# A state-space stage whose matrix products take a fixed place behind the large products

## The chip, the core and the metric

The kernel runs on one core of a Trainium2 chip. The metric is the device time of one execution in microseconds (us), here the median of three runs. A core has five instruction queues that run on their own and meet at semaphores: TensorE (PE, matrix products), VectorE (DVE), ScalarE (ACT), GpSimd (POOL) and SyncE (SP, which here only issues transfers, and waits for what each of them needs before it goes on to the next).

## The reference

One layer of a decoder block, 512 tokens of width 1024, everything in float32:

```
h = RMSNorm(x);  u = h @ W_in                     # 11512 columns: three mixers and three gates
y_A = DSA(u_A) @ W_br_A                           # attention over the 256 top keys
y_B = NSA(u_B) @ W_br_B                           # compressed, selected and window attention
y_C = SSD(u_C) @ W_br_C                           # state-space mixer, Mamba-2
x = x + (sig(g_A)*y_A + sig(g_B)*y_B + sig(g_C)*y_C) @ W_out
x = x + relu(RMSNorm(x) @ W_1)^2 @ W_2
```

The state-space mixer works on 4 chunks (c) of 128 tokens, 4 groups (g) and 8 heads of 64 channels in a group:

```
cb     = C[chunk] @ B[chunk].T                    # 128x128, one for each group
lmat   = exp(a_cum_i - a_cum_j), j <= i           # 128x128 for each head: the decay
y_diag = (cb * lmat) @ (dt * xs)                  # inside the chunk
states = B.T @ (decay * dt * xs)                  # what the chunk hands on
h_c+1  = h_c * chunk_decay + states               # the recurrence over chunks
y_off  = (C @ h_c) * exp(a_cum)                   # from the chunks before
y      = RMSNorm((y_diag + y_off + xs * D) * silu(z)) * g
```

## The kernel before

Two generators write the program. `main` goes through the latency-bound work: the index scores of DSA, the DSA attention, the state-space stage (`ssd`), the NSA attention. `filler` holds the large products: all columns of `W_in`, then the branch products with `W_br`. Each large product is three matrix instructions of 128x512 (`mm3`, L364 to L367, since a float32 is split into a high and a low half); they are the "products" of this text. `main` yields a price in ns; the loop at the end of `build_kernel` then takes steps of `filler` until their prices make up for it. A stage multiplies its prices by a ratio: R1 for DSA, R3 for the state-space stage, R2 for NSA. Where `main` yields a name instead ("x2"), the filler runs until that part is done. `main` is written with a higher priority (HM), so the scheduler, which puts each engine's instructions into one fixed order by its own estimate of when inputs are ready, may draw an instruction of `main` ahead of filler work written earlier. On the chip each engine then keeps that order.

The filler's gates: the branch products begin once NSA has begun its second group of queries ("att2"), those of the state-space branch once that stage is done ("yc"), the last of the NSA branch (`b1`) once the NSA output has been written and read back: its first half needs "nsa5", its second half "nsa". If the filler stands at a gate, it yields None, and `main` goes on alone.

The state-space stage (L1118 to L1242) has 16 units (g, c), taken in pairs of groups. `stage1` takes buffers and issues the six loads of a unit: E (L1130, 512 KB, the cumulated decay of 8 heads, broadcast to 128 partitions), xs (L1132) and zs (L1134), 256 KB each, and bcx, three tiles of 64 KB (L1136 to L1138). All have two buffers. `stage2` has the product C B (L1145, PSUM "pT", evacuated to cbm by ACT), the mask on E (POOL, L1148), eight exponentials (ACT, L1151), the scaled inputs xt and xw (POOL), and E times cbm (DVE, L1158). `stage3` has the product with the carried state (L1169), the new state (L1176), the eight y products (L1186) and the evacuation yv; four transposes of yv (L1197) follow one unit later. The loop calls `need(i + 2)`, then `stage2(i + 1)`, then `stage3(i)`, so loads are written two units ahead.

The NSA attention (L784 to L1000) has 32 units of four heads: scores (L801, L802), row maximum (DVE, L803), exponentials (ACT, L810), the scaling (DVE, L823), transposes (L837), their evacuation into a high and a low half (ACT L841, DVE L842), the product with V (L849, L850), and every second unit an output (ACT L856, DVE L857, write L858), which `load_y` (L714 to L716) reads back and splits for `b1`.

Of the kernel before, what the change touches and what calls it, by code (L numbers as in the profile page):

```python
# [7 lines left out]
F32 = mybir.dt.float32  # L8
# [26 lines left out]
R0, R1, R2, R3 = 1000.0, 1.5, 2.5, 0.5  # L35


def build_kernel(ctx, tc, A, out):
    nc = tc.nc
# [35 lines left out]
    bt_d = scratch("bt_d", [S, 512])  # L75
# [288 lines left out]
    def mm3(o, lh, ll, rh, rl, first, last):  # L364
        pe.matmul(o, lh, rh, start=first, stop=False)  # L365
        pe.matmul(o, lh, rl, start=False, stop=False)  # L366
        pe.matmul(o, ll, rh, start=False, stop=last)  # L367
# [750 lines left out]
    def ssd(sv, ratio):  # L1118
# [5 lines left out]
        def stage1(g, c):  # L1124
            u = U()
            u.g, u.c = g, c
            rows = slice(c * 128, c * 128 + 128)
            cols = slice(g * 512, g * 512 + 512)
            u.E = sp.tile([128, 8, 128], F32, name="E", bufs=2)
            nc.sync.dma_start(u.E, bcast_rows(ac_d, c * 32 + g * 8, 8))  # L1130
            u.xs = sp.tile([128, 512], F32, name="xs", bufs=2)
            nc.sync.dma_start(u.xs, xs_d[rows, cols])  # L1132
            u.zs = sp.tile([128, 512], F32, name="zs", bufs=2)
            nc.sync.dma_start(u.zs, zs_d[rows, cols])  # L1134
            u.b = sp.tile([128, 3, 128], F32, name="bcx", bufs=2)
            nc.sync.dma_start(u.b[:, 0], bt_d[rows, g * 128:g * 128 + 128])  # L1136
            nc.sync.dma_start(u.b[:, 1], BC_d[g * 128:g * 128 + 128, rows])
            nc.sync.dma_start(u.b[:, 2], BC_d[512 + g * 128:512 + g * 128 + 128, rows])  # L1138
            return u

        def stage2(u):
# [3 lines left out]
            pe.matmul(p[:, :128], u.b[:, 1], u.b[:, 2], start=True, stop=True)  # L1145
# [17 lines left out]
        def stage3(u):  # L1163
# [3 lines left out]
            if c:  # L1167
                po = ps("sc", [128, 512])
                pe.matmul(po, u.b[:, 2], hst[g], start=True, stop=True)  # L1169
# [4 lines left out]
            if c < 3:  # L1174
                pst = ps("pT", [128, 512])
                pe.matmul(pst, u.b[:, 0], u.xw, start=True, stop=True)  # L1176
# [8 lines left out]
            for h in range(8):  # L1185
                pe.matmul(py[:, h * 64:h * 64 + 64], u.E[:, h], u.xt[:, h * 64:h * 64 + 64], start=True, stop=True)  # L1186
# [7 lines left out]
            def tr():  # L1194
                pt = ps("pT", [128, 4, 128])
                for k in range(4):
                    pe.transpose(pt[:, k], yv[:, k * 128:k * 128 + 128], ident)  # L1197
# [18 lines left out]
        yield from need(0)  # L1216
        yield from need(1)
        yield from stage2(us[0])
        for i in range(16):
# [6 lines left out]
            yield from stage3(us[i])  # L1226
        TR.pop()()
# [362 lines left out]
```

## Time and profile before

| | |
|---|---|
| median of 3 runs | 1424.58 us (1424.15 to 1425.3) |
| the profiled execution's own time | 1425.82 us |
| its span in the trace | 1424.1 us |
| PE busy, of the span | 1365.5 us, 96% |
| DVE, ACT, POOL busy | 1044.6, 712.6, 347.0 us |
| mean granted clock of PE | 0.987 |
| moved by the transfers | 195.92 MB, 138 GB/s over the span |

An instruction's busy time on PE overlaps that of the next, so a busy PE says only that it never stood still. What it cost to stand still is in the idle time, given in brackets in the timeline and in the list of waits, with the instruction that ended it. The granted clock is the share of full speed: 1.00 is 2.4 GHz, 0.50 is 1.2 GHz.

### The profile page before, as it was taken

The numbers are of one execution on the slowest core, as the hardware profiler recorded it, in microseconds if no ns is written. First come the engines' busy times: TensorE is split into PE (matmuls) and PEld (weight loads), VectorE is DVE, ScalarE is ACT, GpSimd is POOL, SyncE is SP. The second block draws the span as 40 slices with busy tenths as digits, with TensorE's granted clock in tenths as the row PEclk, the third lists the DMA queues.
The fourth block names the chain that finished last, engine by engine and source line by source line (L and its number), as shares of the span: only waits on it lengthen the run. The fifth ranks groups of instructions, "written<-read, shape, count | busy, mean of one in ns | idle before, by whom it ended". The sixth has DMA issues, their size and how long they took to land.

```text
span 1424.1 us, 19720 instructions
## 1 busy us (share of the span) xinstructions
PE 1365.5 (96%) x6760; PEld 1126.1 (79%) x6760; DVE 1044.6 (73%) x1959; ACT 712.6 (50%) x1433; POOL 347.0 (24%) x294
## 2 busy tenths in 40 slices
PE   5989899999999999999999999999799999999998
PEld 4878688888877877788888867787579888888887
DVE  4599966798977665468568898888655777869841
ACT  5445245677666566455555544646433444443420
POOL 5454201111046576202003533524100000000000
PEclk9999899999999999999999999999999999999999
DMA  6236465544576778844326743424464433241221
GB/s 204 73 102 139 130 189 144 137 113 125 133 224 190 215 202 223 232 139 122 96 79 193 228 134 87 136 67 126 158 212 127 126 111 110 87 136 45 67 89 52
DMA packets 232097, 195.92 MB, mean 138 GB/s; under 512 B 17200, under 2 KB 183484, under 8 KB 231996
## 3 DMA queue, kind: packets, MB, share of 16 engines
q1 hardware_dynamic: 226524, 183.12, 44.3%
q0 software_dynamic: 4608, 8.39, 2.2%
q10 hardware_dynamic: 864, 3.15, 0.6%
q8 instruction: 53, 0.87, 0.3%
q14 instruction: 48, 0.39, 0.1%
HBM read 157.85 MB, written 36.77 MB: 137 GB/s over the span
## 4 chain that ended last, share of the span: by engine, by line
PE 71%; DVE 10%; DMA 7%; issue 4%; ACT 4%; POOL 2%; SPq 2%; DVEq 0%; ACTq 0%; POOLq 0%
PE pj L365 17%; PE pj L366 17%; PE pj L367 16%; PE sc L366 3%; PE sc L367 3%; PE sc L365 3%; PE pT L837 2%; PE sc L802 2%; PE sc L801 2%; PE pv L850 2%; PE pv L849 2%; DVE wlo L159 1%; DMA gld<-g_d 1%; SPq L525 1%; DMA E<-ac_d 1%
## 5 line engine op out<-in xcount | busy, mean ns | idle before, releaser
L158 ACT ACTIVATE whi<-wraw 128x1024 fp32r<-128x1024 f32 (+3 forms) x188 | 181.7, 975 | 210.8 <-PE pj L366 124.3
L159 DVE TENSOR_TENSOR wlo<-wraw,whi 128x1024 fp32r<-128x1024 f32 (+1 forms) x164 | 194.5, 1188 | 77.4 <-ACT whi L158 75.6
L365 PE MATMUL pj<-hTh,whi 128*128 128x512 f32 x384 | 154.9, 403 | 0.2 <-DVE cacc L732 0.2
L367 PE MATMUL pj<-hTh,wlo 128*128 128x512 f32 x384 | 153.5, 400 | 0.0
L366 PE MATMUL pj<-hTl,whi 128*128 128x512 f32 x384 | 153.3, 399 | 0.0
L365 PE MATMUL pj<-whi,hTh 128*128 128x512 f32 (+2 forms) x352 | 141.6, 404 | 8.3 <-DVE stk L435 3.2
L810 ACT ACTIVATE p<-p,nb,rs 128x256 f32<-128x256 f32 (+3 forms) x192 | 123.2, 645 | 50.6 <-DVE nb L808 50.6
L366 PE MATMUL pj<-wlo,hTh 128*128 128x512 f32 (+2 forms) x352 | 140.0, 398 | 0.8 <-POOL wlo L159 0.8
L367 PE MATMUL pj<-whi,hTl 128*128 128x512 f32 (+2 forms) x352 | 138.5, 394 | 0.0
L365 PE MATMUL pj<-yh,whi 128*128 128x512 f32 x256 | 103.0, 406 | 9.4 <-ACT yh L715 7.7
L366 PE MATMUL pj<-yl,whi 128*128 128x512 f32 x256 | 102.2, 399 | 0.4 <-DVE yl L716 0.4
L367 PE MATMUL pj<-yh,wlo 128*128 128x512 f32 x256 | 101.9, 399 | 0.0
L366 PE MATMUL pj<-h2l,whi 128*128 128x512 f32 (+1 forms) x256 | 96.3, 376 | 0.0
L367 PE MATMUL pj<-h2h,wlo 128*128 128x512 f32 (+1 forms) x256 | 96.2, 376 | 0.0
L365 PE MATMUL pj<-h2h,whi 128*128 128x512 f32 (+1 forms) x256 | 96.1, 376 | 0.0
L821 POOL TENSOR_TENSOR p<-p,rc 128x256 f32<-128x256 f32 (+3 forms) x48 | 38.2, 795 | 219.7 <-DVE rc L816 63.2
L365 PEld LDWEIGHTS pj<-whi,hTh 128*128 128x128 f32 x352 | 68.3, 194 | 22.5 <-issue 6.4
L365 PEld LDWEIGHTS pj<-hTh,whi 128*128 128x128 f32 x384 | 72.3, 188 | 16.4 <-issue 1.7
L367 PEld LDWEIGHTS pj<-hTh,wlo 128*128 128x128 f32 x384 | 72.2, 188 | 15.2 <-issue 1.2
L366 PEld LDWEIGHTS pj<-hTl,whi 128*128 128x128 f32 x384 | 72.3, 188 | 15.0 <-issue 1.7
L841 ACT ACTIVATE pth<-pT 128x512 fp32r<-128x512 f32 x95 | 55.0, 593 | 56.8 <-PE pT L837 54.8
L366 PEld LDWEIGHTS pj<-wlo,hTh 128*128 128x128 f32 x352 | 68.4, 194 | 14.9 <-issue 2.2
(357 smaller groups left out, 3372.9 us busy)
## 6 DMA issues: line engine op xcount, KB each, us to landing
wraw<-in_w_in_dram SPq DMA_DIRECT2D x84, 512.0 KB, 4.5
wraw<-in_w_ff_dram SPq DMA_DIRECT2D x40, 512.0 KB, 4.1
gld<-g_d SPq DMA_DIRECT2D x48, 256.0 KB, 3.3
qd<-in_w_ff_dram SPq DMA_DIRECT2D x24, 512.0 KB, 3.9
q_d<-qev SPq DMA_DIRECT2D x128, 64.0 KB, 2.6
qu<-q_d POOLq DMA_DIRECT2D x32, 256.0 KB, 3.7
E<-ac_d SPq DMA_DIRECT2D x16, 512.0 KB, 4.9
wraw<-in_w_br_ssd_dram SPq DMA_DIRECT2D x16, 512.0 KB, 3.8
```

Of the source, the lines that this page charges most:

```text
L158: act.activation(hi[:, :m], r[:, :m], AF.Copy)
L159: (pool if i < NP else dve).tensor_tensor(lo[:, :m], r[:, :m], f(hi[:, :m]), op=ALU.subtract)
L365: pe.matmul(o, lh, rh, start=first, stop=False)
L366: pe.matmul(o, lh, rl, start=False, stop=False)
L367: pe.matmul(o, ll, rh, start=False, stop=last)
L801: pe.matmul(s_[:, h % w, :n], u.q[:, h], kh[:, :n], start=True, stop=False)
L802: pe.matmul(s_[:, h % w, :n], u.q[:, h], kl[:, :n], start=False, stop=True)
L810: act.activation(u.p[h][:, :n], u.p[h][:, :n], AF.Exp, bias=u.nb[:, h:h + 1], scale=rs8[:, u.b, u.h0 + h:u.h0 + h + 1], accum_out=u.sm[:, ...
L821: pool.tensor_tensor(u.p[h][:, :n], u.p[h][:, :n], bc(rc[:, h:h + 1], [128, n]), op=ALU.mult)
L837: pe.transpose(pt[:, h], u.p[h][:, kb * 128:kb * 128 + 128], ident)
L841: act.activation(ph, ptf, AF.Copy)
L849: pe.matmul(o, vk, ph0, start=st, stop=False)
```

## The change

R3 goes from 0.5 to 2.0: for every price of the state-space stage four times as much of the filler is written beside it. Every matrix instruction of the stage is queued on PE behind the last product that had been written by then (`tc.issue_after`, an order of issue, no wait for completion). The loads of a unit are written in a new order, bcx first, then E; xs and zs move to `load_xz`, which for unit i + 2 is called after `stage3(i)`. E and bcx get three buffers.

```diff
-R0, R1, R2, R3 = 1000.0, 1.5, 2.5, 0.5
+R0, R1, R2, R3 = 1000.0, 1.5, 2.5, 2.0
...
-        pe.matmul(o, ll, rh, start=False, stop=last)
+        LF[0] = pe.matmul(o, ll, rh, start=False, stop=last)
+
+    LF = [None]
+
+    def paced():
+        return tc.issue_after(LF[0].ins if hasattr(LF[0], "ins") else LF[0])
...
-            u.E = sp.tile([128, 8, 128], F32, name="E", bufs=2)
+            u.b = sp.tile([128, 3, 128], F32, name="bcx", bufs=3)
+            nc.sync.dma_start(u.b[:, 1], BC_d[g * 128:g * 128 + 128, rows])
+            nc.sync.dma_start(u.b[:, 2], BC_d[512 + g * 128:512 + g * 128 + 128, rows])
+            nc.sync.dma_start(u.b[:, 0], bt_d[rows, g * 128:g * 128 + 128])
+            u.E = sp.tile([128, 8, 128], F32, name="E", bufs=3)
             nc.sync.dma_start(u.E, bcast_rows(ac_d, c * 32 + g * 8, 8))
+            return u
+
+        def load_xz(u):
...
             u.xs = sp.tile([128, 512], F32, name="xs", bufs=2)
             nc.sync.dma_start(u.xs, xs_d[rows, cols])
             u.zs = sp.tile([128, 512], F32, name="zs", bufs=2)
             nc.sync.dma_start(u.zs, zs_d[rows, cols])
...
             p = ps("pT", [128, 512])
-            pe.matmul(p[:, :128], u.b[:, 1], u.b[:, 2], start=True, stop=True)
+            with paced():
+                pe.matmul(p[:, :128], u.b[:, 1], u.b[:, 2], start=True, stop=True)
...
             for h in range(8):
-                pe.matmul(py[:, h * 64:h * 64 + 64], u.E[:, h], u.xt[:, h * 64:h * 64 + 64], start=True, stop=True)
+                with paced():
+                    pe.matmul(py[:, h * 64:h * 64 + 64], u.E[:, h], u.xt[:, h * 64:h * 64 + 64], start=True, stop=True)
...
             yield from stage3(us[i])
+            if i + 2 < 16:
+                load_xz(us[i + 2])
```

The products of L1169 and L1176 and the transposes of L1197 are put into `paced()` in the same way, and `load_xz` is called for the first two units ahead of `stage2(us[0])`.

The order of PE at the first two units of the stage. L1145 is C B of a unit, L1176 its new state, L1186 its y products, L1197 transposes of yv, L743 transposes of the convolution; L365 to L367 are products. Before:

```order
L1186 MATMUL sc<-xt,E 128x64 x8
...
L365 MATMUL pj<-hTh,whi 128x512
L1145 MATMUL pT<-bcx 128x128
L1186 MATMUL sc<-xt,E 128x64 x7
L1197 MATMUL pT<-ident,yv 128x128 x4
L1186 MATMUL sc<-xt,E 128x64
L1169 MATMUL sc<-hst,bcx 128x512
L743 MATMUL pF<-ident,craw 128x128 x4
L366 MATMUL pj<-hTl,whi 128x512
```

After the change, with the line numbers of the changed kernel (L1154 is C B, L1198 the y products, L1179 the product with the carried state, L1210 the transposes, L1187 the new state):

```order
L1198 MATMUL sc<-xt,E 128x64 x8
L1154 MATMUL pT<-bcx 128x128
L365 MATMUL pj<-hTh,whi 128x512
...
L365 MATMUL pj<-hTh,whi 128x512
L1198 MATMUL sc<-xt,E 128x64 x8
L1179 MATMUL sc<-hst,bcx 128x512
L366 MATMUL pj<-hTl,whi 128x512
L367 MATMUL pj<-hTh,wlo 128x512
L365 MATMUL pj<-hTh,whi 128x512
L1210 MATMUL pT<-ident,yv 128x128 x4
```

C B of the unit after next stands ahead of the products instead of behind them, and 13 products instead of 22 lie between the first two groups of y. Over the whole stage, counted in the two orders from the first y to the last transpose (L1235), 464 products lie between before and 517 after: 53 more.

The transfers on SP in the middle of the stage. Before, the six loads of one unit come after each other as their buffers allow:

```order
L1201 DMA yc_d<-yev 128x4x128
L1134 DMA zs<-zs_d 128x512
L1132 DMA xs<-xs_d 128x512
L1136 DMA bcx<-bt_d 128x128
L1137 DMA bcx<-BC_d 128x128
L1138 DMA bcx<-BC_d 128x128
L750 DMA xs_d<-xev 128x4x128
L142 DMA wraw<-in_w_in_dram 128x8x128
L1130 DMA E<-ac_d 128x1024
```

After (L1134 to L1136 load bcx, L1138 E, L1145 xs, L1147 zs, L1214 writes yc):

```order
L1214 DMA yc_d<-yev 128x4x128
L1138 DMA E<-ac_d 128x1024
L1134 DMA bcx<-BC_d 128x128
L1135 DMA bcx<-BC_d 128x128
L1136 DMA bcx<-bt_d 128x128
L142 DMA wraw<-in_w_in_dram 128x2x512
L1147 DMA zs<-zs_d 128x512
L1134 DMA bcx<-BC_d 128x128
```

The loads of bcx run up to a unit ahead of the others, and zs and xs come last.

The end of the NSA attention on PE. L801 and L802 are scores, L837 transposes, L849 and L850 the products with V, L989 those of the compressed branch. Before, the last V products lie among the products of `b0` and of the first half of `b1`:

```order
L849 MATMUL pv<-pth,v_w_313 128x512
L837 MATMUL pT<-ident,p 128x128 x2
L365 MATMUL pj<-yh,whi 128x512
L837 MATMUL pT<-ident,p 128x128 x2
L850 MATMUL pv<-ptl,v_w_313 128x512
L366 MATMUL pj<-yl,whi 128x512
L367 MATMUL pj<-yh,wlo 128x512
L365 MATMUL pj<-yh,whi 128x512
L849 MATMUL pv<-pth,v_s_311 128x512
L365 MATMUL pj<-yh,whi 128x512
```

After (L842 transposes, L854 and L855 V products, L994 compressed branch):

```order
L842 MATMUL pT<-ident,p 128x128 x4
L854 MATMUL pv<-pth,v_s_311 128x512
L842 MATMUL pF<-ident,p 128x128 x4
L855 MATMUL pv<-ptl,v_s_311 128x512
L842 MATMUL pT<-ident,p 128x128 x4
L994 MATMUL pv<-cph,vz 128x128 x4
L854 MATMUL pv<-pth,v_w_313 128x512
L855 MATMUL pv<-ptl,v_w_313 128x512
L854 MATMUL pv<-pth,v_s_311 128x512
L855 MATMUL pv<-ptl,v_s_311 128x512
L365 MATMUL pj<-yh,whi 128x512 x2
L366 MATMUL pj<-yl,whi 128x512
```

The last product of `b0` now stands 52 instructions ahead of the first of `b1`, and all 52 are NSA's: 18 scores, 16 transposes, 8 of the compressed branch and 10 with V. All 96 products of `b1` stand behind the last product with V; before it was 84 of them.

## Rows read from the trace of the kernel before

**Rows 1.** The page's first part: busy us, share of the span and instructions of each engine (PEld: PE's weight loads).

```profile
PE 1365.5 (96%) x6760; PEld 1126.1 (79%) x6760; DVE 1044.6 (73%) x1959; ACT 712.6 (50%) x1433; POOL 347.0 (24%) x294
```

**Rows 2.** Busy time of PE, PE's weight loads, DVE, ACT and POOL in stretches of the span, then the granted clock, the transfers' share of the 16 DMA engines and GB/s: the state-space stage (398 to 605 us, and its later part alone), then the later part of the NSA attention.

```profile
398.00:605.00 207.00, 197.81 (x1008) 158.12 (x1007) 130.26 (x153) 125.17 (x325) 119.51 (x93) 0.98 0.77 216
460.00:605.00 145.00, 139.57 (x714) 111.87 (x713) 83.91 (x102) 85.16 (x224) 82.54 (x65) 0.96 0.80 217
...
800.00:900.00 100.00, 94.44 (x457) 73.99 (x456) 88.67 (x171) 50.21 (x98) 43.30 (x32) 1.00 0.47 136
900.00:1000.00 100.00, 97.46 (x514) 80.47 (x515) 84.58 (x220) 53.88 (x133) 37.13 (x33) 1.00 0.35 101
```

**Rows 3.** What PE waited for in the state-space stage (390 to 610 us): the waiting line, what ended the wait, us in total, times, the longest.

```profile
PE pT L1145 <- DMA bcx<-BC_d: 6.0, 5, 2.1
PE sc L1186 <- DVE E L1158: 1.7, 1, 1.7
PE pT L1145 <- ACT zs L1192: 0.8, 1, 0.8
PE pT L1176 <- ACT cbm L1147: 0.7, 2, 0.4
```

**Rows 4.** Stretches of 5 us around the two longest of these waits, columns as in rows 2.

```profile
505.00:510.00 5.00, 3.34 (x17) 2.87 (x17) 3.93 (x6) 5.00 (x13) 0.81 (x1) 0.79 0.62 178
510.00:515.00 5.00, 5.00 (x15) 3.42 (x14) 5.00 (x6) 4.07 (x12) 2.98 (x2) 0.53 0.97 266
...
530.00:535.00 5.00, 5.00 (x31) 4.25 (x30) 1.40 (x3) 1.43 (x5) 4.16 (x5) 1.00 0.99 284
...
540.00:545.00 5.00, 4.01 (x13) 2.73 (x14) 1.55 (x3) 1.78 (x6) 3.13 (x3) 0.70 0.88 252
```

**Rows 5.** The timeline of PE at the two waits: start, duration, instruction, and in brackets the idle time before it and what ended it.

```profile
507.35 2.40 PE L1186 MATMUL sc<-xt,E 128*128 128x64 f32 x12 [1.66 <-DVE E L1158]
540.99 0.46 PE L1145 MATMUL pT<-bcx 128*128 128x128 f32 x2 [2.12 <-DMA bcx<-BC_d]
```

**Rows 6.** The instructions on the tile E (count, then ns min/median/max) and the time from issue to landing of its loads.

```profile
L1151 ACT ACTIVATE E<-E,sv_nac x128: 382/387/408, 403.3 to 577.3; 128x128 f32<-128x128 f32 x128
L1148 POOL TENSOR_SCALAR_AFFINE_SELECT E<-E x16: 1086/1092/2190, 402.2 to 574.1; 128x1024 f32<-128x1024 f32 x16
L1158 DVE TENSOR_TENSOR E<-E,cbm x16: 1210/1226/2061, 409.1 to 582.1; 128x1024 f32<-128x1024 f32 x16
DMA to landing us min/median/max: 3.7/4.9/6.4
```

**Rows 7.** The same time for the three loads of bcx.

```profile
DMA to landing us min/median/max: 1.8/3.4/5.8
```

**Rows 8.** The timeline of PE at the end of the NSA attention.

```profile
1003.00 0.50 PE L849 MATMUL pv<-pth,v_w 128*128 128x512 f32 x1 [1.46 <-ACT pth L841]
...
1008.78 0.39 PE L850 MATMUL pv<-ptl,v_s 128*128 128x512 f32 x1
1016.35 1.22 PE L365 MATMUL pj<-yh,whi 128*128 128x512 f32 x2 [7.18 <-ACT yh L715]
...
1018.23 0.63 PE L365 MATMUL pj<-yh,whi 128*128 128x512 f32 x1
1018.65 0.63 PE L366 MATMUL pj<-yl,whi 128*128 128x512 f32 x1
...
1020.14 0.40 PE L367 MATMUL pj<-yh,wlo 128*128 128x512 f32 x1
1020.37 0.40 PE L366 MATMUL pj<-yl,whi 128*128 128x512 f32 x1
```

**Rows 9.** The chain of waits in order of time across that gap: start, us, what.

```profile
1009.20 0.60 ACT yt L856
...
1009.83 0.69 DVE yt L857
...
1010.54 2.45 DMA yb_d<-yt
...
1013.01 2.64 DMA yr<-yb_d
...
1015.67 0.64 ACT yh L715
```

**Rows 10.** Single instructions of an NSA unit of 128 keys in the timeline, by engine: scores and transposes on PE, an exponential and the evacuation on ACT, the scaling and the low half on DVE.

```profile
978.74 0.22 PE L801 MATMUL sc<-kh_w,qu 128*128 128x128 f32 x1
...
979.14 0.69 PE L837 MATMUL pT<-ident,p 128*128 128x128 f32 x4
...
994.45 0.48 ACT L810 ACTIVATE p<-p,nb,rs 128x128 f32<-128x128 f32 x1
...
994.93 0.48 ACT L810 ACTIVATE p<-p,nb,rs 128x128 f32<-128x128 f32 x1
...
1005.33 0.58 ACT L841 ACTIVATE pth<-pT 128x512 fp32r<-128x512 f32 x1
...
1002.77 0.82 DVE L823 TENSOR_SCALAR p<-p,rc 128x128 f32<-128x128 f32 x3
1003.52 0.68 DVE L842 TENSOR_TENSOR ptl<-pF,pth 128x512 fp32r<-128x512 f32 x1
```

More of the change, by code (lines that the diff above doesn't have):

```diff
@@ L1127, in stage1 @@
             rows = slice(c * 128, c * 128 + 128)
-            cols = slice(g * 512, g * 512 + 512)
-            u.E = sp.tile([128, 8, 128], F32, name="E", bufs=2)
+            u.b = sp.tile([128, 3, 128], F32, name="bcx", bufs=3)
[3 more added lines that the diff above has]
+            u.E = sp.tile([128, 8, 128], F32, name="E", bufs=3)
             nc.sync.dma_start(u.E, bcast_rows(ac_d, c * 32 + g * 8, 8))
+            return u
+        def load_xz(u):
+            rows = slice(u.c * 128, u.c * 128 + 128)
+            cols = slice(u.g * 512, u.g * 512 + 512)
             u.xs = sp.tile([128, 512], F32, name="xs", bufs=2)
@@ L1134, in stage1 @@
             nc.sync.dma_start(u.zs, zs_d[rows, cols])
[L1135 to L1139, printed above, removed]
         def stage2(u):
@@ L1168, in stage3 @@
                 po = ps("sc", [128, 512])
-                pe.matmul(po, u.b[:, 2], hst[g], start=True, stop=True)
+                with paced():
+                    pe.matmul(po, u.b[:, 2], hst[g], start=True, stop=True)
                 t1 = sp.tile([128, 512], F32, name="t1", bufs=2)
@@ L1175, in stage3 @@
                 pst = ps("pT", [128, 512])
-                pe.matmul(pst, u.b[:, 0], u.xw, start=True, stop=True)
+                with paced():
+                    pe.matmul(pst, u.b[:, 0], u.xw, start=True, stop=True)
                 hn = sp.tile([128, 512], F32, name="hst", bufs=4)
@@ L1185, in stage3 @@
             for h in range(8):
-                pe.matmul(py[:, h * 64:h * 64 + 64], u.E[:, h], u.xt[:, h * 64:h * 64 + 64], start=True, stop=True)
+                with paced():
+                    pe.matmul(py[:, h * 64:h * 64 + 64], u.E[:, h], u.xt[:, h * 64:h * 64 + 64], start=True, stop=True)
                 if h % 4 == 3:
@@ L1195, in tr @@
                 pt = ps("pT", [128, 4, 128])
-                for k in range(4):
-                    pe.transpose(pt[:, k], yv[:, k * 128:k * 128 + 128], ident)
+                with paced():
+                    for k in range(4):
+                        pe.transpose(pt[:, k], yv[:, k * 128:k * 128 + 128], ident)
                 ev = sp.tile([128, 4, 128], F32, name="yev", bufs=2)
@@ L1216, in ssd @@
         yield from need(0)
+        load_xz(us[0])
         yield from need(1)
+        load_xz(us[1])
         yield from stage2(us[0])
```

## The prediction

> **What bounds the kernel now.** I read the page's busy shares first, then the time in stretches, then what PE waited for, then the timeline at its gaps. PE is busy for 1365.5 of 1424.1 us [rows 1]. The change adds and removes no matrix instruction, so it can win only what PE stands still or runs slowly, and lose by making it stand still elsewhere. In the state-space stage, 398 to 605 us, PE is busy 197.8 of 207 us: 9.2 us idle [rows 2]. The list of waits accounts for all of it: 6.0 us at C B (L1145) for bcx, 1.7 us at y for E, 0.8 us at C B for ACT and 0.7 us at the new state [rows 3]. Beside that the granted clock in 460 to 605 us is 0.96 [rows 2], which is 0.04 x 145 = 5.8 us of full-speed time. Most of it lies in three stretches, 0.79, 0.53 and 0.70 of 5 us, together 1.05 + 2.35 + 1.5 = 4.9 us [rows 4], and each of the two falls comes at a wait: 1.66 us before 507 us, 2.12 us before 541 us [rows 5]. I count 4.5 us as work lost to the clock, since part of the slow time is idle anyway. So at most 9.2 + 4.5 = 13.7 us can be won in the stage.
>
> The Trainium skill, "TensorE: Matmul & The Clock Gate", says in "Terms" that the penalty is the throttled time times one minus the ratio of the clocks; the rows say the same here, as a clock of 0.53 in a stretch without idle time is about 4.7 us at half speed and 2.35 us lost.
>
> **The change, part by part.**
>
> *Loads and buffers.* bcx is waited for because its three loads stand last in a unit's six on SP, and two buffers let them start only when the products of the unit two back are done. They land 1.8 to 5.8 us after issue, median 3.4 [rows 7]. With three buffers and the first place they are issued about a unit earlier, and a unit lasts 207 / 16 = 13 us. That is more than the longest landing, so the 6.0 us should go. The E path is 4.9 us of landing, 1.1 of masking, 8 x 0.39 = 3.1 of exponentials and 1.2 on DVE, 10.3 us [rows 6], in a buffer that now comes free a unit earlier: the 1.7 us go too, unless ACT or POOL is late. The waits of 0.8 and 0.7 us for ACT are not addressed by a buffer; products written between may cover them.
>
> What can be late next is xs and zs. They keep two buffers, are written after `stage3(i)`, and stand behind E and bcx in SP's queue; SP holds everything behind a load whose buffer is not free. The units are also closer in the beginning: counted in the two orders, 84 products lie between the first y of the first six units against 151 before, so a unit there takes some 17 x 0.23 = 3.9 us of products (spacing of rows 8) and about 5 us of its own instead of 12. POOL, with six instructions near 1.05 us a unit (that of E is 1.09 [rows 6]), and ACT, with 3.1 us of exponentials and half as much again, still fit into 9 us, but without much room. Transfers ran at 217 GB/s with a share of 0.80 and reached 284 GB/s in one stretch [rows 2, 4]; 1.2 MB of loads and 0.25 MB of output every 9 us are 161 GB/s, and weights and convolution bring that to about 230. I leave 2.5 of the 9.2 us of waits, between 0 and 8: minus 6.7. With few waits the clock should fall rarely: I leave 1.2 of 4.5, minus 3.3.
>
> *The order of issue.* The matrix instructions keep their number and the y products their weights; a y that now stands between products costs no more. Cost nothing, with the product beside it as cover, and up to 1 us either way if a weight load is no longer hidden.
>
> *R3.* 53 products more are written into the stage. At a spacing of 0.23 us [rows 8] that is 12.2 us of PE, which the stage gets longer by and the NSA attention shorter by: nothing in sum. But NSA now runs out of cover at its end. Before, only 84 of 96 products of `b1` came after the last product with V, and PE stood still 7.18 us while the last output went to memory and back [rows 8]. After, 52 NSA instructions follow on each other with nothing between.
>
> I work that end out from T, the end of the last product of `b0`. Before, everything but 84 products was done at 1008.78 + 0.39 = 1009.2 us [rows 8]. Take off the idle 1.5 us there, the 12 products more (2.8 us) and the 52 instructions: 18 scores at 0.1 (four from 978.74 to 979.14 us), 24 transposes or like sizes at 0.12, 10 with V at 0.23, in all 7.0 us [rows 8, 10]. T is 997.9 us.
>
> From T the chain goes through ACT and DVE. Evacuating and scaling the unit in hand takes DVE to T + 1.7, its transposes to 2.2, the output's evacuation and the next row maxima to 3.7. Then come three groups of four exponentials at 0.48 [rows 10]: the first 3.7 to 5.8, the second, after its maxima, 7.0 to 9.0, an evacuation of 0.6, the third to 11.7. Scaling with its reciprocal 1.2, transposes 0.5, the two evacuations 0.58 and 0.68 one after another, V and its waits 1.0 [rows 10]: T + 15.7. Output 0.60 + 0.69 to 17.1, write 2.45, read 2.64, split 0.64 [rows 9]: T + 23. The output before it is ready at T + 14.1, so `b1` begins at 20, and its first 12 products, eight of them at the 0.42 us that PE took after the gap before [rows 8], end at T + 24.4 = 1022.3 us. They hide the last read. Before, the second half began at 1016.35, and its own slow start cost 8 x 0.2 = 1.6 us more [rows 8], which the first half now pays: 1018.0. The end of NSA costs 4 us, between 0 (the NSA instructions drawn forward leave less of the chain) and 11 (below).
>
> *The rest of NSA.* Its waits, 5.6 and 2.5 us in 800 to 1000 us [rows 2], fall anew in the other order; nothing, within 2 us either way.
>
> Sum: -6.7 - 3.3 + 4 = -6.0 us. The profiled execution took 1425.82 us, its span and 1.7 us around it; the sum gives 1419.8 us. The median is 1.24 us below that execution, so I predict 1418.6 us. Its own range is 1413 to 1422.
>
> **Rivals.**
>
> *The end of NSA takes back more than the stage gives (slower).* For it: the chain has no product beside it, DVE still has the filler's last work before it, some four instructions of 0.68 (size of those in rows 10), 2.7 us; PE is so thinly used that it may run all of it at half clock, which doubles three groups of transposes and the V products on the path, 3 x 0.5 + 0.9 = 2.4 us; and write and read may wait for the weights' transfers, 1.5 us more. With 4 that makes 10.6. If the stage then gives only 6 of its 10, the sum is +4.6 and the time 1429.2 us. It decides as soon as the end costs more than the stage wins. Against: the prices in my sum come from a stretch in which filler work lay between, so they carry some of this already [rows 9, 10].
>
> The Trainium skill's page on the clock gate, Part 1, says that the default is the throttled state and that activity lifts it; by that rule the bare end stays at half speed. The trace agrees for the gap before, 0.63 us for a product after 7.18 us of standing still against 0.40 us later [rows 8]; for a thinly used PE no row shows it.
>
> *The wait only changes its load (no change).* xs or E, late in the dense first units, stops y or the new state for as long as bcx stopped C B. For it: two buffers, the last place in SP's queue, 284 GB/s at the peak [rows 4]. Against: after the first six units 30 to 48 products lie between the units, counted in the order. The stage gives 3 us, the end costs 4: 1425.6 us.
>
> *Everything goes.* The stage gives all 13.7 us and NSA's end costs nothing, as the scheduler draws it forward: 1410.9 us.
>
> That the change doesn't do what it says I rule out: the orders show the products between and the loads moved.
>
> **How the numbers follow.** My forecast 0.54, the bare end of NSA 0.20, the changed wait 0.18, everything 0.08. A difference of 0.2%, 2.8 us, is about what a measurement of this kernel can tell from no change. The forecast lies on the fast side for 0.50 of its 0.54, with all of the last case and 0.02 of the changed wait: faster 0.60. No change: 0.04, 0.13 of the changed wait, 0.03 of the bare end, 0.20. Slower: 0.17 and 0.03 of the changed wait, 0.20. The range reaches from the last case to the slow one, 1410 to 1429.
>
> **What would show it.** Right: no wait of C B for bcx in the list, PE idle 2 to 4 us in the stage, a clock of 1.00 through it, the stage's end some 3 us later than 605; then a gap pattern from about 993 us on, with PE waiting for ACT's exponentials and evacuations, and `b1`'s second half starting without a wait near 1016 (1022.3 less what the stage won). Wrong: waits of y or of the new state for xs or E of over 5 us, or a fall of the clock in the first six units; more than 8 us between the 12 products of `b1`'s first half and what the chain above gives.

## The result, and the profile after

The changed kernel takes 1443.06 us (four runs, 1437.98 to 1446.83) against 1424.37 us for the kernel before: a ratio on record of 1.0113, interval 1.0075 to 1.0150 (the two medians alone give 1.0131). It is slower, and the prediction had the sign wrong and the time outside its range. The profiled execution is the slowest of the four, 1446.83 us with a span of 1445.1 us, 21.0 us more than that of before.

PE is busy 12.3 us longer than in [rows 1], though it runs the same 6760 instructions:

```profile
PE 1377.8 (95%) x6760; PEld 1134.5 (79%) x6760; DVE 1046.0 (72%) x1959; ACT 712.7 (49%) x1433; POOL 349.2 (24%) x294
```

The next views cut both spans at the same landmarks: the state-space stage (first C B to the last of its transposes), the NSA stage in three parts (cut before the 337th and the 841st of its 896 matrix instructions that are not large products, which I call its first part, its middle and its last part, up to the last product with V), the way to the first product of W_out, the rest. First before, columns as in [rows 2]:

```profile
405.00:599.00 194.00, 185.91 (x952) 148.61 (x953) 125.12 (x148) 120.01 (x315) 114.49 (x87) 0.97 0.77 215
599.00:754.00 155.00, 155.00 (x800) 130.55 (x798) 105.59 (x277) 83.13 (x178) 21.64 (x26) 1.00 0.40 117
754.00:977.00 223.00, 215.05 (x1089) 174.12 (x1089) 193.26 (x444) 119.34 (x262) 89.48 (x71) 1.00 0.47 138
977.00:1009.00 32.00, 29.90 (x146) 23.23 (x144) 26.54 (x63) 17.03 (x47) 13.95 (x13) 1.00 0.51 155
1009.00:1040.00 31.00, 22.42 (x87) 17.05 (x87) 19.59 (x28) 12.56 (x17) 0.00 (x0) 0.89 0.51 166
1040.00:1421.00 381.00, 380.34 (x1783) 318.55 (x1781) 255.18 (x289) 140.43 (x170) 2.23 (x4) 1.00 0.33 103
```

Then the changed kernel:

```profile
406.00:613.00 207.00, 196.20 (x1014) 156.91 (x1013) 124.86 (x150) 124.50 (x324) 120.06 (x89) 0.99 0.76 214
613.00:774.00 161.00, 161.00 (x827) 135.38 (x825) 111.37 (x284) 85.02 (x183) 27.02 (x31) 1.00 0.45 134
774.00:1005.00 231.00, 215.73 (x1071) 173.86 (x1071) 196.37 (x438) 117.76 (x256) 93.68 (x72) 0.99 0.42 122
1005.00:1028.00 23.00, 18.01 (x69) 13.29 (x67) 16.67 (x60) 12.49 (x41) 4.17 (x6) 0.68 0.28 91
1028.00:1059.00 31.00, 26.19 (x98) 19.84 (x99) 21.08 (x30) 14.14 (x19) 0.00 (x0) 0.86 0.56 184
1059.00:1442.00 383.00, 380.83 (x1784) 318.72 (x1782) 255.17 (x289) 139.94 (x169) 2.23 (x4) 1.00 0.32 102
```

Every large product is one instruction each of L365, L366 and L367, so the same windows for L366 alone count them (times three). The two parts of the NSA stage that matter, before:

```profile
754.00:977.00 223.00, 77.18 (x194) 36.53 (x194) 1.00 0.47 138
977.00:1009.00 32.00, 12.08 (x30) 5.65 (x30) 1.00 0.51 155
```

and in the changed kernel:

```profile
774.00:1005.00 231.00, 76.72 (x190) 36.18 (x190) 0.99 0.42 122
1005.00:1028.00 23.00, 1.63 (x4) 0.76 (x4) 0.68 0.28 91
```

To compare stretches that hold different numbers of products I take off the products at 381 / (3 x 584) = 0.217 us, their spacing in the last stretch. What is left is the time "beyond its products". The middle: 223 - 582 x 0.217 = 96.7 us before, 231 - 570 x 0.217 = 107.3 us after, +10.6. The last part: 32 - 90 x 0.217 = 12.5 us, then 23 - 12 x 0.217 = 20.4 us, +7.9. The state-space stage is 13 us longer, 53 products, and beyond them unchanged (+0.5 us, by the table below). So 18.5 of the 21 us arise in the NSA stage, and the stage that the change rewrote gained nothing.

In that stage the list of waits shows what stands there now, against [rows 3]:

```profile
PE pF L520 <- DVE qev L524: 5.3, 4, 2.8
PE pT L1210 <- DVE hst L1193: 2.3, 1, 2.3
PE sc L1198 <- DVE E L1167: 2.0, 2, 1.6
PE pT L1187 <- POOL xw L1165: 0.7, 1, 0.7
PE pF L748 <- ACT xev L750: 0.4, 1, 0.4
```

The wait for bcx (6.0 us) is gone, though its loads land no faster (median 3.6 us for 3.4 in [rows 7]). 10.7 us of waits stand where 9.2 stood, now for DVE: the transposes of the large products' own results (L520) wait for the single buffer pF, others for hst and E. The clock did recover, as predicted, but for one fall that follows the wait of 2.3 us for hst (it ends at 453.29 us), 0.91 over 440 to 460 us:

```profile
460.00:605.00 145.00, 139.68 (x728) 113.01 (x727) 82.50 (x103) 81.60 (x206) 73.43 (x54) 1.00 0.76 206
440.00:460.00 20.00, 17.38 (x84) 13.42 (x85) 16.23 (x20) 13.57 (x37) 17.94 (x15) 0.91 0.75 230
```

Over the middle and the last part of the NSA stage PE now waits more for DVE's scaling of p (7.7 us for 2.1) and for its low halves ptl (2.2 us for 0.2), but not for the row maxima mx. Before, 753 to 1010 us:

```profile
PE sc L801 <- DVE mx L803: 2.9, 6, 1.3
PE pF L837 <- DVE p L823: 1.8, 3, 0.9
PE pT L837 <- DVE p L823: 0.3, 1, 0.3
```

After, 773 to 1028 us:

```profile
PE pT L842 <- DVE p L828: 5.5, 8, 1.1
PE pF L842 <- DVE p L828: 2.2, 3, 1.1
PE pv L855 <- DVE ptl L847: 2.2, 3, 1.2
PE sc L806 <- DVE mx L808: 2.1, 6, 0.4
```

The end, where products are missing, runs at half clock (columns as in [rows 2]):

```profile
1000.00:1010.00 10.00, 9.54 (x52) 7.85 (x50) 9.72 (x23) 5.56 (x15) 2.93 (x4) 1.00 0.33 103
1010.00:1020.00 10.00, 7.21 (x28) 5.59 (x28) 7.14 (x33) 4.90 (x19) 1.81 (x3) 0.65 0.43 144
1020.00:1030.00 10.00, 6.26 (x18) 4.06 (x18) 5.49 (x15) 4.68 (x14) 0.81 (x2) 0.50 0.20 60
1030.00:1037.00 7.00, 6.19 (x14) 4.34 (x15) 2.17 (x4) 2.52 (x4) 0.00 (x0) 0.50 0.35 104
```

PE's timeline there answers to [rows 8]:

```profile
1008.28 0.40 PE L367 MATMUL pj<-yh,wlo 128*128 128x512 f32 x1
...
1011.69 0.64 PE L842 MATMUL pT<-ident,p 128*128 128x128 f32 x3 [0.90 <-DVE p L828]
...
1018.28 1.07 PE L842 MATMUL pT<-ident,p 128*128 128x128 f32 x4
...
1030.81 1.22 PE L365 MATMUL pj<-yh,whi 128*128 128x512 f32 x2 [2.88 <-ACT yh L720]
...
1035.67 0.63 PE L367 MATMUL pj<-yh,wlo 128*128 128x512 f32 x1
1036.19 1.08 PE L365 MATMUL pj<-yh,whi 128*128 128x512 f32 x2
```

Four transposes take 1.07 us where [rows 10] had 0.69, and all twelve products of `b1`'s first half last 0.63 us.

### The profile page after: what moved, and what is told of

The parts are those of the page before. It is cut to its first block, busy times and chain, and to the rows that moved or that the text cites. A ratio compares the mean times of both kernels' runs of the same rounds, so it can differ in the third digit from the quotient of the medians.

```text
span 1445.1 us, 19688 instructions
## 1 busy us (share of the span) xinstructions
PE 1377.8 (95%) x6760; PEld 1134.5 (79%) x6760; DVE 1046.0 (72%) x1959; ACT 712.7 (49%) x1433; POOL 349.2 (24%) x294
## 4 chain that ended last, share of the span: by engine, by line
PE 66%; DVE 14%; DMA 8%; ACT 4%; issue 3%; POOL 3%; SPq 1%; DVEq 0%; POOLq 0%; ACTq 0%
PE pj L365 16%; PE pj L367 15%; PE pj L366 15%; DMA gld<-g_d 3%; PE sc L367 3%; PE sc L365 3%; PE sc L366 3%; PE pT L842 2%; DMA wraw<-in_w_in_dram 2%; DVE wlo L159 2%; PE sc L807 1%; PE sc L806 1%; ACT p L815 1%; DVE p L828 1%; PE pv L854 1%
## 5 line engine op out<-in xcount | busy, mean ns | idle before, releaser
L365 PE MATMUL pj<-hTh,whi 128*128 128x512 f32 x384 | 157.6, 410 | 0.2 <-DVE cacc L737 0.2
L367 PE MATMUL pj<-hTh,wlo 128*128 128x512 f32 x384 | 154.6, 403 | 0.0
L366 PE MATMUL pj<-hTl,whi 128*128 128x512 f32 x384 | 154.5, 402 | 0.0
L365 PE MATMUL pj<-whi,hTh 128*128 128x512 f32 (+2 forms) x352 | 142.3, 406 | 8.3 <-DVE stk L440 3.2
L366 PE MATMUL pj<-wlo,hTh 128*128 128x512 f32 (+2 forms) x352 | 140.0, 398 | 0.8 <-POOL wlo L159 0.8
L367 PE MATMUL pj<-whi,hTl 128*128 128x512 f32 (+2 forms) x352 | 139.4, 397 | 0.0
L365 PE MATMUL pj<-yh,whi 128*128 128x512 f32 x256 | 104.0, 412 | 5.6 <-ACT yh L720 3.4
L366 PE MATMUL pj<-yl,whi 128*128 128x512 f32 x256 | 103.7, 406 | 1.4 <-POOL yl L721 1.4
L367 PE MATMUL pj<-yh,wlo 128*128 128x512 f32 x256 | 103.6, 405 | 0.0
L366 PE MATMUL pj<-h2l,whi 128*128 128x512 f32 (+1 forms) x256 | 96.3, 376 | 0.0
L367 PE MATMUL pj<-h2h,wlo 128*128 128x512 f32 (+1 forms) x256 | 96.2, 376 | 0.0
L365 PE MATMUL pj<-h2h,whi 128*128 128x512 f32 (+1 forms) x256 | 96.1, 376 | 0.0
L365 PEld LDWEIGHTS pj<-hTh,whi 128*128 128x128 f32 x384 | 72.5, 189 | 16.5 <-issue 2.9
L365 PEld LDWEIGHTS pj<-whi,hTh 128*128 128x128 f32 x352 | 68.5, 195 | 21.5 <-issue 5.9
L367 PEld LDWEIGHTS pj<-hTh,wlo 128*128 128x128 f32 x384 | 72.5, 189 | 15.5 <-issue 1.7
L366 PEld LDWEIGHTS pj<-hTl,whi 128*128 128x128 f32 x384 | 72.7, 189 | 15.1 <-issue 2.3
L846 ACT ACTIVATE pth<-pT 128x512 fp32r<-128x512 f32 x95 | 54.8, 593 | 59.1 <-PE pT L842 56.8
L366 PEld LDWEIGHTS pj<-wlo,hTh 128*128 128x128 f32 x352 | 68.8, 195 | 13.5 <-POOL wlo L159 1.1
```

The costliest lines, as they stand in the source:

```text
L367: LF[0] = pe.matmul(o, ll, rh, start=False, stop=last)
L846: act.activation(ph, ptf, AF.Copy)
```

## The experiments

The table has every kernel's median and ratio to the kernel before on the same chip (before: 1424 to 1429 us there), then, from one profiled execution each, the number of large products in a part and the part's time beyond them (us), worked out from the starts of single instructions, so that they differ a little from the rounded windows. The state-space column counts from the first C B, 25 products ahead of the first y. Kernels with the same counts in the last two columns repeat within 2 us there (107.4 to 109.4 and 19.7 to 20.3). The kernels ran on several chips, so a difference of two medians can hold up to 4 us of the chip; the ratios do not.

Theory A: the ratio takes products from the NSA stage, which loses by their lack. Theory B: the loads cost. Theory C: in the state-space stage waits are only swapped. D (pacing costs) and F (VectorE's chain is the floor of the NSA stage's second part) came later.

| kernel | us | ratio, 95% | state-space | NSA first | NSA middle | NSA last |
|---|---|---|---|---|---|---|
| before | 1424.4 | | 489 / 88.0 | 458 / 54.8 | 585 / 96.1 | 88 / 13.0 |
| changed | 1443.1 | 1.0075–1.0150 | 542 / 88.5 | 485 / 55.3 | 570 / 107.8 | 11 / 20.3 |
| e1_loads | 1433.6 | 1.0022–1.0059 | 386 / 89.4 | 487 / 60.9 | 633 / 97.0 | 114 / 10.1 |
| e2_ratio | 1435.6 | 1.0033–1.0071 | 489 / 88.0 | 466 / 55.0 | 581 / 101.9 | 72 / 14.7 |
| e3b_paced_ratio | 1449.5 | 1.0126–1.0176 | 542 / 93.6 | 485 / 55.3 | 570 / 109.4 | 11 / 19.7 |
| e5_ratio_loads | 1432.4 | 1.0008–1.0048 | 397 / 91.9 | 501 / 59.8 | 602 / 96.6 | 120 / 10.9 |
| e4_paced_loads | 1426.5 | 0.9974–1.0015 | 348 / 91.0 | 473 / 60.1 | 572 / 94.4 | 120 / 9.7 |
| e7_r3_14 | 1434.2 | 1.0032–1.0070 | 446 / 95.0 | 491 / 55.3 | 595 / 96.8 | 88 / 16.7 |
| e6_r2_220 | 1452.7 | 1.0163–1.0225 | 542 / 88.5 | 485 / 55.3 | 544 / 110.5 | 49 / 19.1 |
| e8_pv | 1464.2 | 1.0235–1.0296 | 656 / 84.2 | 485 / 55.3 | 570 / 107.4 | 11 / 20.2 |
| e10_pv_late | 1441.1 | 1.0052–1.0105 | 542 / 87.5 | 485 / 55.3 | 570 / 107.4 | 11 / 20.1 |
| e10_e4_pv | 1431.3 | 0.9982–1.0030 | 363 / 96.8 | 485 / 56.5 | 618 / 93.8 | 119 / 14.4 |
| e9_after_act | 1431.4 | 1.0001–1.0030 | 542 / 88.9 | 476 / 55.3 | 563 / 89.8 | 39 / 18.2 |
| e9_before_act | 1438.4 | 1.0054–1.0091 | 489 / 87.2 | 483 / 55.2 | 588 / 100.0 | 60 / 17.5 |
| e13_after_half | 1435.2 | 1.0035–1.0075 | 542 / 88.8 | 469 / 56.4 | 572 / 95.9 | 25 / 17.0 |
| e13_before_half | 1425.7 | 0.9967–1.0000 | 489 / 86.5 | 456 / 55.8 | 579 / 93.2 | 96 / 14.2 |
| e12_act_r3_14 | 1426.6 | 0.9967–1.0004 | 446 / 95.3 | 490 / 55.4 | 584 / 90.5 | 100 / 13.8 |
| e12_act_r3_05 | 1422.7 | 0.9936–0.9975 | 348 / 94.0 | 494 / 58.4 | 526 / 88.4 | 131 / 9.8 |

**The parts of the change.** Four kernels take it apart. Pacing alone, at the old ratio and with the old loads, gives the program of before, instruction for instruction on all five engines, so it changes nothing.

e1_loads, the loads and buffers alone:

```diff
-R0, R1, R2, R3 = 1000.0, 1.5, 2.5, 2.0
+R0, R1, R2, R3 = 1000.0, 1.5, 2.5, 0.5
...
     def paced():
-        return tc.issue_after(LF[0].ins if hasattr(LF[0], "ins") else LF[0])
+        return ExitStack()
```

> Only the loads: three buffers for E and bcx, the decay loads ahead, xs and zs behind stage3; the ratio stays 0.5 and nothing is paced. In program order the state-space stage then holds 361 large products (464 before, 517 in the changed kernel) and the NSA stage 1235 ahead of its last V (1132 before, 1067 changed), with 5 instructions of other kinds behind the last product of the first block (51 changed). Theory A, the loss comes from the products that the NSA stage lacks: about 1418 us, 6 under before, since the six waits for bcx (some 6 us) go and the NSA stage is covered. Theory B, the new loads cost by themselves (they put E and xs into each other's way on SP's queue): 1430 or more, with waits for E, xs or zs in the stage. Theory C, waits for loads are only swapped for waits on VectorE in this stage: 1423 to 1426.

1433.6 us, slower than before: theory A missed by 15 us, C by 8. B's number (1430 or more) was met, but its signs (waits for E, xs or zs) are absent except for 0.9 us at E. The stage waits for hst, yv and xt, and the first part of the NSA stage took 6.1 us more beyond its products.

e2_ratio (`R3` 0.5 to 2.0 in the kernel before):

> Only the ratio, 0.5 to 2.0; loads and buffers as before, nothing paced. The order has 464 large products in the state-space stage as before, 1120 in the NSA stage ahead of its last V (12 fewer) and 21 instructions of other kinds in a row at its end instead of 7. Theory A (products that the NSA stage lacks): 1425 to 1428, the 12 products' worth at the end. Theory B (the loads are what costs) and theory C: 1424, as before. A rival, that the ratio alone makes the loss: 1440.

1435.6 us, between A and its rival: 16 products fewer in the last part and 5.8 us more in the middle, in another order.

e3b_paced_ratio (the changed kernel with the loads and two buffers of before):

> Pacing and the ratio 2.0, with the loads and two buffers of before. The counts of the changed kernel: 517 large products in the state-space stage, 1067 in the NSA stage ahead of its last V, 51 instructions of other kinds at its end. Theory A: as slow as the changed kernel or slower, 1443 to 1450, with the NSA stage's loss (about 19 us against before) whole and the waits for bcx back. Theory B (loads): 1424 to 1430. Theory C: the NSA loss as A has it, and a stage that is 0 to 2 us shorter or longer than that of the changed kernel, since waits for VectorE and for loads change places.

1449.5 us: A held; B fell, and so did C, as this stage is 5.1 us longer than the changed kernel's and not within 2. Here the bcx wait is back, and longer:

```profile
PE pT L1151 <- DMA bcx<-BC_d: 10.7, 9, 3.5
```

Its stage has 93.6 us beyond its products for 88.5 with the new loads, and its whole time is 6.4 us above the changed kernel's. So in the paced order the loads are worth 5 to 6 us. The stage's zero is then a sum: pacing at the ratio 2.0 with the old loads costs the stage 5.6 us (93.6 for 88.0, which e2_ratio without pacing keeps), and the new loads give 5.1 us back.

e5_ratio_loads (the changed kernel with `paced` as in e1_loads):

> The changed kernel without pacing (ratio 2.0, new loads, three buffers). The order has 372 large products in the state-space stage, 1224 in the NSA stage ahead of its last V, 5 instructions of other kinds at its end. Theory A: 1418 to 1420, nearly that of the loads alone, though the ratio is 2.0. Theory B (loads): 1440 as the changed kernel. A rival, that the ratio makes the loss whatever the order: 1440 too; the waits in the stage tell these apart.

1432.4 us: without pacing the ratio puts few products into the stage (397), and some 11 of the 19 us are gone. Neither number of theory A was met, B's 1440 neither.

**Back towards the old ratio.** e4_paced_loads (`R3` 2.0 to 0.5) and e7_r3_14 (`R3` 1.4) are the changed kernel with that one number changed.

> The changed kernel with the old ratio 0.5 (paced, new loads, three buffers). The order has 323 large products in the state-space stage, 1165 in the NSA stage ahead of its last V and 192 behind it, and the NSA's last V stands among products. Theory A, the loss of the changed kernel is its ratio, by the products that its NSA stage lacks: 1422 to 1430. Theory D, pacing costs by itself (a fixed order behind the products makes PE wait for VectorE): 1435 or more, with the stage's time beyond its products 5 us over that of before.

> The changed kernel with the ratio 1.4 in place of 2.0: 421 large products in the state-space stage (517), 1175 in the NSA stage ahead of its last V (1067), 15 instructions of other kinds at its end (51). Theory A: the NSA stage's time beyond its products falls by most of the 20 us that the changed kernel lost there, to within 5 us of before; whole kernel 1426 to 1432. Theory D: 1438 or more.

At 0.5 the loss is gone: 1426.5 us, no difference from before; A held and D fell. At 1.4 it is 1434.2 us, about halfway and between the two theories. The middle of the NSA stage is back at 94 to 97 us beyond its products in both; at 1.4 the last part still costs 16.7 us, and the state-space stage needs 95.0 us for 88.0, more than the 5 us that D named, for reasons that no run separates.

e6_r2_220 leaves the stage and spreads the NSA's products thinner:

```diff
-R0, R1, R2, R3 = 1000.0, 1.5, 2.5, 2.0
+R0, R1, R2, R3 = 1000.0, 1.5, 2.2, 2.0
```

> The changed kernel with the NSA stage's own ratio 2.2 in place of 2.5: the same 517 large products in the state-space stage, 1079 (1067) in the NSA stage ahead of its last V, spread thinner, and 31 instructions of other kinds at its end instead of 51. Theory A with the weight on the bare end: 6 to 8 us less than the changed kernel, 1435 to 1437. Theory A with the weight on the middle (what the end gains is lost where the products are thinner): 1441 to 1445.

1452.7 us, worse than either expected. 38 products more in the last part gained 1.2 us there, and the middle, with 26 fewer, lost 2.7. The medians lie 9.6 us apart, the profiled executions only 4.3; the rest of these 4.3 us falls between the last V and W_out, where 84 products cover the last output's way through memory again instead of 96 (32.5 us for 30.7). Thinning the products does not mend the end.

**The waits of the stage.** e8_pv gives pF's transposes a second buffer in PSUM (`FT[0]` is true while `ssd` is written):

```diff
     def ps(tag, shape, dt=F32, bufs=2):
-        if tag == XT[0]:
+        if tag == "pF" and FT[0]:
+            FT[1] += 1
+            tag = "pv" if FT[1] % 2 else "pF"
+        elif tag == XT[0]:
```

> The changed kernel with a second PSUM buffer for the large products' own transposes during the state-space stage (pF and the idle pv by turns), whose wait for VectorE's qev was the largest in that stage (5.3 us of 10.7). Theory C1, that wait is a buffer's and goes: 4 to 5 us less than the changed kernel, 1438 to 1439. Theory C2, VectorE is late and the wait moves to its other results (E, hst) behind which the transposes stood: 1442 to 1444, with the stage's idle time still 9 us or more.

1464.2 us. The stage did gain 4.3 us beyond its products, but the stretch in front of it held 114 products fewer and lost 21 us. PE's waits from 200 to 403 us are 16.8 us there and 0.2 us in the changed kernel to 406 us. Of these, 3.7 us (all after 350 us) are waits of the filler's transposes, drawn ahead into the DSA stage, for pv; how the others come from the edit is not shown. From 350 to 403 us:

```profile
PE pv L751 <- ACT xev L753: 1.9, 2, 1.2
PE pv L751 <- DVE yt L865: 1.8, 1, 1.8
```

e10_pv_late sets the switch `FT[0] = 1 <= i < 14` ahead of `stage3(us[i])`; e10_e4_pv does so at `R3` 0.5.

> The changed kernel with the second PSUM buffer (pf and pv by turns) for the large products' transposes from the second to the fourteenth unit of the state-space stage alone, so that the DSA stage before it keeps pv. The earlier trial had a stage 4.3 us shorter beyond its products, idle 3.9 us for 10.8, and lost 21 us in front of the stage. Theory C1: that loss goes and the stage's gain stays, 1438 to 1440. Theory C2: the stage gains nothing without it, 1443.

1441.1 us. The qev wait falls from 5.3 to 0.8 us, but waits for cbm, xt and cacc come with 3.4 us. PE stands still 7.7 us for 10.8, at a granted clock of 0.98 for 0.99 (2 us), and the stage wins 1.0 us; the whole lies between C1 and C2. Waits of PE, 405 to 610 us:

```profile
PE pT L1213 <- DVE hst L1196: 2.1, 2, 1.5
PE pT L1190 <- ACT cbm L1159: 1.2, 1, 1.2
PE pj L368 <- DVE cacc L740: 1.1, 1, 1.1
PE pT L1190 <- POOL xt L1165: 1.1, 1, 1.1
PE pF L523 <- DVE qev L527: 0.8, 1, 0.8
```

> The same second buffer with the changed kernel at the old ratio 0.5 (1426.5 us without it): 338 large products in the state-space stage, 1222 in the NSA stage ahead of its last V, 120 behind it. The stage's time beyond its products was 91 us with 13.5 us idle. Theory C1: 4 to 6 us less, 1421 to 1423, faster than the kernel before. Theory F adds that the 57 further products in the NSA stage lengthen it by their full 0.22 us each, since it is above its floor, and the whole by nothing. Theory C2: 1426 as without it.

1431.3 us, and the stage needs 96.8 us beyond its products: C1 fell. At neither ratio was the buffer what held the stage.

**VectorE in the NSA stage.** e9_after_act and e9_before_act move one p scaling of each NSA unit, in the changed kernel and in the one before:

```diff
+            elif h == 2 and u.gate is not None:
+                act.activation(u.p[h][:, :n], u.p[h][:, :n], AF.Copy, scale=rc[:, h:h + 1])
             else:
                 dve.tensor_scalar(u.p[h][:, :n], u.p[h][:, :n], rc[:, h:h + 1], None, op0=ALU.mult)
```

> The changed kernel with one of the three p scalings that each NSA unit does on VectorE moved to ScalarE (about 21 of 0.61 us in the units behind 774 us; ScalarE is idle for 124 of the 254 us there). Theory F, the second part of the NSA stage has a floor of about 255 us that VectorE's chain sets, whatever number of large products it holds (255.4 us with 673 before, 254.3 us with 581 changed): the floor falls, by 5 to 12 us, and the whole kernel by as much, to 1431 to 1438. Theory A, PE lacks products there and nothing else: no change, 1442 to 1445.

> The kernel before with the same p scaling moved to ScalarE. Theory F: PE has 10 us of idle time in those 255 us, and what of it waits for VectorE goes: 2 to 6 us less than before, 1418 to 1422, a smaller gain than in the changed kernel, where 20 us are idle. Theory A: 1424 as before, or slower.

The changed kernel gained 11.6 us (1431.4 us), within F's band. DVE is busy 202 us over the middle and the last part for 213 without the move (sums of the windows), and together they are 15 us shorter, 239 for 254:

```profile
768.00:980.00 212.00, 206.74 (x1069) 171.60 (x1068) 184.18 (x419) 125.00 (x271) 88.53 (x72) 1.00 0.45 131
980.00:1007.00 27.00, 21.35 (x97) 16.60 (x95) 18.09 (x56) 16.01 (x49) 6.71 (x8) 0.81 0.40 117
```

The kernel before lost 9 us by the same edit (1438.4 against 1429.0 us), where a gain was expected. Its order changed with it: 60 products in the last part instead of 88, and 3.9 us more in the middle. The last part is in line with the others. In its middle VectorE's busy time did not fall, 193.8 of 228 us for 193.3 of 223, so the new order put other work of VectorE's there; which, and why the middle lost, is open.

e13_after_half and e13_before_half cut DVE's work and keep the order more nearly; they leave most of p unscaled:

```diff
-                dve.tensor_scalar(u.p[h][:, :n], u.p[h][:, :n], rc[:, h:h + 1], None, op0=ALU.mult)
+                m = n if u.gate is None else 64
+                dve.tensor_scalar(u.p[h][:, :m], u.p[h][:, :m], rc[:, h:h + 1], None, op0=ALU.mult)
```

> The changed kernel with VectorE's p scalings of the NSA units cut to 64 columns of each (the rest of p is left unscaled, so the attention outputs differ): some 60 instructions of 0.61 us fall to about 0.2 us, 25 us less of VectorE's 213 us in the second part of the NSA stage. The order stays nearly that of the changed kernel: 597 (581) large products in that part, 25 (14) in its last sixteenth, 45 (51) instructions of other kinds at its end. Theory F (VectorE's chain is the floor): that part, 254 us, falls by 10 to 20 us, whole kernel 1425 to 1433. Theory A (a bare end and too few products, in the order alone): at most 3 us less, 1440 or more.

> The kernel before with the same cut (p partly unscaled, so the attention outputs differ): 675 (673) large products in that part of the NSA stage, 7 (7) instructions of other kinds at its end. Theory F: its 10 us of idle time there shrink by half or more and it gets 4 to 8 us faster, less than the changed kernel does, because its products, which take 146 us there, begin to set the length. Theory A: 1424 to 1429, as before.

The changed kernel fell by 7.9 us, just short of F's band and far from A's. Its middle needs 95.9 us beyond its products, as much as that of before; its bare last part still 17.0. Windows of the two parts:

```profile
772.00:992.00 220.00, 211.07 (x1076) 172.26 (x1076) 186.89 (x435) 118.24 (x256) 89.82 (x72) 1.00 0.44 128
992.00:1015.00 23.00, 19.92 (x84) 14.49 (x82) 16.71 (x59) 13.19 (x41) 5.84 (x7) 0.74 0.44 137
```

The kernel before gained less, 2.4 us (0 to 4.7 by the interval), and its two parts together 1 us, 254 for 255:

```profile
752.00:971.00 219.00, 213.20 (x1088) 176.63 (x1087) 183.67 (x440) 119.82 (x261) 90.43 (x70) 0.98 0.48 140
971.00:1006.00 35.00, 32.45 (x154) 26.03 (x152) 25.88 (x68) 17.50 (x49) 16.07 (x14) 0.95 0.56 164
```

So VectorE's work sets the length of the middle in the changed kernel, and hardly in the kernel before. The number of products does not tell the two apart: e4_paced_loads has 572 in its middle, two more than the changed kernel, and 94.4 us beyond them for 107.8. Of these, 115 belong to W_in, and VectorE is busy 181 of 219 us, where it was 196 of 231:

```profile
735.00:954.00 219.00, 211.15 (x1080) 174.53 (x1079) 180.98 (x434) 120.24 (x263) 74.56 (x62) 0.99 0.48 138
```

Between before and changed VectorE's work hardly differs (193 and 196 us). What differs is how long VectorE itself waits for the loads of the gates (gld), over the middle and the last part together 10.4 us before (754 to 1009 us) and 17.1 after (773 to 1028 us):

```profile
L1319 DVE SCALAR_TENSOR_TENSOR gld<-gld,rtok 128x512 f32<-128x512 f32 x16 | 12.4, 779 | 10.4 <-DMA gld<-g_d 10.4
L1336 DVE SCALAR_TENSOR_TENSOR gld<-gld,rtok 128x512 f32<-128x512 f32 x16 | 12.5, 782 | 17.1 <-DMA gld<-g_d 17.1
```

No run changes these loads alone, and e1_loads has 16.7 us of that wait in a middle of 97.0 us, so their share in the loss is open.

**A version that beats both.** e12_act_r3_14 and e12_act_r3_05 are e9_after_act with `R3` 1.4 and 0.5.

> The changed kernel with one p scaling per unit on ScalarE (1431.4 us at the ratio 2.0) and the ratio 1.4: 421 large products in the state-space stage (517), 684 in the second part of the NSA stage (602). Theory F: the state-space stage is 21 us shorter by its 96 products less what its waits take (6 us were taken at this ratio without the move), the NSA stage's second part grows by about 10 us, together 4 to 6 us less: 1425 to 1428. Theory A: the same sign; no telling of the two here, but faster than 1431 by both. If it is 1431 or more, products are worth the same wherever they stand once VectorE is relieved.

> The same with the old ratio 0.5: 323 large products in the state-space stage, 665 in the second part of the NSA stage, 206 behind its last V. Without the move it took 1426.5 us, its NSA stage with 9.5 us idle. Theory F: 3 to 6 us less, 1421 to 1424, faster than the kernel before. Theory A: 1426, as without the move.

1426.6 and 1422.7 us, inside the bands of theory F. The first does not differ from the kernel before (0.9967 to 1.0004). The second is faster than the kernel before by 0.44% (interval 0.25 to 0.64%), on the same chip 1422.7 against 1428.1 us. The window of its NSA stage's last part shows no idle time of PE and no half clock:

```profile
943.00:982.00 39.00, 39.00 (x195) 32.56 (x194) 26.81 (x65) 17.38 (x47) 10.57 (x10) 1.00 0.33 92
```

## Why the prediction was wrong

**The stage's waits, -6.7 us.** The mechanism held in part: the bcx wait left, and the loads are worth 5.1 us of stage in the paced order (e3b_paced_ratio against the changed kernel). What failed is "I leave 2.5 of the 9.2 us of waits": 10.7 us stood there after. The step looked for a successor among the loads (E, xs, zs) and not at the engine that works on PE's results. With PE no longer stopped by bcx, DVE was next, and when its largest wait was removed (e10_pv_late), the stage won 1.0 us. "The order of issue" was put at nothing too: e3b_paced_ratio shows that pacing at this ratio, with the old loads, costs the stage 5.6 us. The rival "the wait only changes its load" was near, but the new waits were for an engine and not for a load. Of the signs of "wrong", waits for xs or E of over 5 us did not appear (2.0 us for E); a fall of the clock in the first six units did, 0.91 over 440 to 460 us, as the sixth unit's first y comes at 461.7 us.

**The stage's clock, -3.3 us.** Right in size: the stage's granted clock rose from 0.97 to 0.99, 0.03 x 194 = 5.8 us lost before and 0.01 x 207 = 2.1 after, 3.7 us less. PE's idle time there took 2.7 of it back (8.1 us before, 10.8 after).

**R3, "nothing in sum".** The moved products did cost what they were said to, 53 in the stage. But the step took them off the NSA stage at full price. That the NSA stage gets shorter by 0.217 us a product is true only where PE is what limits it. Middle and last part together took 255 us with 673 products before and 254 us with 581 after: the 92 products that left them gave back 1 us of the 20 that they are worth. These 19 us are the same as those of the next two steps, seen from the other side.

**The end of NSA, +4 us.** The mechanism was right (PE waiting for p, exponentials and evacuations, `b1`'s second half starting without a wait), the size was not: 7.9 us. The chain from the last product of `b0` to the end of `b1`'s first half took 1036.2 - 1008.7 = 27.5 us where 24.4 was worked out. Of these 3 us, 1.0 are the first half's products, twelve at half speed and not eight; the other 2 fell before them, where transposes and V took about 1.5 times as long at half clock (1.07 us for 0.69, 0.63 for 0.40) and PE waited for p (0.90 us at 1011.69); how the 2 us divide between these is not shown. The rival had counted this, the sum had not. The rival "the bare end takes back more", with its 10.6, was the nearest of all, though its 1429.2 us falls 14 short. In the runs this cost goes with the number of products in the last part: about 20 us at 11, 17 to 19 at 25 to 60, 13 to 15 at 72 to 100, 10 to 11 at 114 to 131 (16.7 at 88 in e7_r3_14 and 14.4 at 119 in e10_e4_pv stand out). No run changes that number alone.

**"The rest of NSA. Nothing, within 2 us either way."** This is the largest miss. It cost 10.6 to 11.7 us, enough alone to turn the sign (-6 + 11); the stage's 10 us would have been, too. I had read 5.6 and 2.5 us of idle time in [rows 2] as waits that fall anew, and not asked what they wait for: in the same rows DVE is busy 88.67 of 100 us in 800 to 900, so it has little slack. e13_after_half shows it: with less work for DVE and 2 products more the middle is back at 95.9 us. The number of products is not the reason by itself: e4_paced_loads has 572 and 94.4 us. What in the changed order makes DVE the limit is open (its waits for gld are the nearest sign).

In sum: a stage of 0 (for -10), a middle of +11, an end of +8, and 2 us after it (383 for 381 us in the last stretch) that no run explains.

## What to carry to other kernels

Moving filler from one stage to another is not free in sum: take its price off the stage it leaves only if that stage is limited by the engine that runs it, and look at how busy the next engine is there before writing zero. When a wait on a load is removed, ask what the engines behind that one still owe; here VectorE's results were waited for instead. Order and ratios act together: pacing alone moved nothing, the loads alone and the ratio alone each cost some 6 to 8 us, and the version that won keeps pacing and loads, leaves the ratio and takes work off VectorE.

## What the hardware showed

A PE that is used thinly, not only one that stands still, ran at the lower of the two levels: 0.50 granted, 1.2 GHz, from 1020 to 1030 us with PE busy 6.26 of 10 us and, ahead of its last wait, none longer than 1.21 us. It stayed there through the first twelve dense products after 1030.81 us (0.63 us each), and from 1037.12 us on a product took 0.40 us. The prediction had this as a rival, without a row for it.

The Trainium skill, "TensorE: Matmul & The Clock Gate", Part 1, has the throttled state as the default that activity lifts. The trace agrees here, with 0.50 granted from 1020 to 1037 us.

In the NSA's middle the changed kernel also had two short falls (the granted clock is 0.99 over 774 to 1005 us), where before had none.
